# Feed-forward products of a two-layer transformer block by Strassen's scheme: seven block products for eight, all tokens in one pass over the weights

## The chip, the cores and the metric

The kernel runs on one core of a Trainium2 chip. The metric is device time in microseconds (us) for one execution; the median of three runs of the kernel before is 3087.64 us (3086.25 to 3088.11). Engines are named as in the profile: PE is TensorE (matmuls), PEld its weight loads, DVE is VectorE, ACT ScalarE, POOL GpSimd, SP SyncE (whose queue issues most transfers).

## What is computed

Two layers over 1024 latent tokens and 256 context tokens of width 1024, all in float32. Each layer has a conditioned norm, one input projection into three kinds of heads, an output projection, and then the part that is changed: a second norm and a gated feed-forward block of inner width 2816 (22 units of 128).

```python
def swiglu(h, w_in, w_out):
    g, u = jnp.split(h @ w_in, 2, axis=-1)
    return (jax.nn.silu(g) * u) @ w_out

# in each layer, after the heads:
x = x + g1[:, None] * y_l
x = x + g2[:, None] * swiglu(modulate(rms_norm(x, norm2[l]), sh2, sc2), w_ffn_in[l], w_ffn_out[l])
if not last:   # the context tokens go through the first layer's block only
    h_ctx = h_ctx + cg1[:, None] * y_c
    h_ctx = h_ctx + cg2[:, None] * swiglu(modulate(rms_norm(h_ctx, norm2[l]), csh2, csc2),
                                         w_ffn_in[l], w_ffn_out[l])
```

So the first layer's block has 1280 tokens, the second's 1024.

## The kernel before

Features lie on the 128 partitions, tokens along the free dimension. Every large product works on operands that are split into a rounded high part and a low part (`split`, L323: ScalarE casts the high part, VectorE subtracts for the low one), and takes three matmuls a k-tile (`part`, L473): high x high, high x low, low x high. A matmul's moving operand is a piece of tokens of one PSUM bank; `SUBS` (L201) gives the pieces: 320 + 320 in the first chunk of 640 tokens, 384 + 256 in the second. In the second layer the second chunk has only 384 latent tokens left, one piece.

The feed-forward block (`ffn`, L1772) goes through the chunks one after the other, first chunk 1, then chunk 0, and reads all of its weights for each. Per chunk it takes the 22 units in three groups (`FGROUPS`, L30). `ffn_group` (L1715) makes gate and up products of a unit, 8 k-tiles each, tanh on ScalarE, two multiplications on VectorE, and a split of the result, which stays in SBUF. `ffn_out` (L1740) then multiplies the 7 or 8 units of the group into each of the 8 output tiles, and VectorE adds each piece to x, which is in SBUF. Weight blocks come by `load_ahead` (L413, 3 raw buffers), are split by `split_ahead` (L431) one block ahead, and are taken by `take` (L460).

The order of every engine's instructions is the order in which the program issues them (`tc.manual_schedule()`). Side work (norms, the conditioning's vector products of this and the next layer) is kept in lanes; `pace` and `fill` (L285 to L301) put in a step of a lane wherever an estimate of each engine's clock says that VectorE and ScalarE are not ahead of TensorE by more than a slack. `finish` (L313) empties the lanes. The norm of chunk 0 for the block runs beside the last group of chunk 1, and in the first layer the next layer's first norm of chunk 1 runs beside the last group of chunk 0; the conditioning for the second layer (`conditioning_beside`, L570) is spread over both chunks of the first layer's block, with two sums on VectorE for each weight block. `running_rinv` (L634) sums the squares for a norm while x is written; `rms_rinv` (L484) makes the factor. `out_proj` (L1674) makes the output projection of one chunk. `final` (L1803) is the last norm.

Of the kernel before, what the change touches and what calls it, by code (L numbers as in the profile page):

```python
# [16 lines left out]
P = 128  # L17
D = 1024
# [11 lines left out]
FGROUPS = ((0, 8), (8, 15), (15, 22))  # L30

# Columns of the packed per-feature constants, per layer.
# [8 lines left out]
class _Line:  # L41
    """An estimate, kept while the kernel is traced, of when each engine is through with its work."""
# [26 lines left out]
    def note(self, engine, name, args, kw):  # L69
# [22 lines left out]
        if engine == "pe":  # L92
            # In columns: the engine has its full clock after a time in which it was busy enough.
# [10 lines left out]
class _Traced:  # L104
    """An engine of the core whose instructions are noted on the line."""
# [15 lines left out]
def hybrid_block_kernel(  # L121
# [28 lines left out]
    # Every engine runs its instructions in the order in which they are traced here.  # L150
# [3 lines left out]
    rp = ctx.enter_context(tc.tile_pool(name="raw", bufs=3))  # L154
    fp = ctx.enter_context(tc.tile_pool(name="full", bufs=27))
# [30 lines left out]
    def act(out, in_, func, **kw):  # L186
        """An activation; Ln and Exp keep to the one table set that has both where they meet."""
# [12 lines left out]
    # The columns (tokens) of each chunk in pieces of one PSUM bank; context: the last.  # L200
    SUBS = {0: ((0, 320), (320, 320)), 1: ((0, 384), (384, 256))}  # L201
# [23 lines left out]
    rope = cp.tile([P, SEQ], F32, name="rope")  # L225
# [14 lines left out]
    xs = dp.tile([2, 4, P, 2, CH], F32, name="xs")  # L240
# [44 lines left out]
    def fill(over=None):  # L285
        """Trace what steps of the lanes the engines have time for before the main stream's next one."""
# [29 lines left out]
    def alternate(main, side, every):  # L316
        """One step of side after every so many of main's."""
# [9 lines left out]
    # The weight blocks [P, k, m] in the order in which they are read: those that are split  # L327
    # (stationary operands of the large products) and the plain ones of the conditioning.
    plan = []

    # The input projection: its units, and the chunks that each pass over one takes.
    UNIT = dict(xr0=0, xr1=1, gg0=2, gg1=3, kv=4, qa0=5, qa1=6, su0=7, su1=8)
# [14 lines left out]
    # Of the conditioning's steps, those beside the first layer's projections, and those that come later.  # L347
    LATE = 8
    N_TICKS = 24 - LATE
    # What of the conditioning is computed beside the first layer's feed-forward: layer and block.  # L350
    BESIDE = [(0, 40), (0, 44)] + [(1, b) for b in range(0, 48, 4)]

    def pieces_of(l, c, name):
        """The pieces in which one unit of a chunk is computed."""
        return 2 if l < DEPTH - 1 or c == 0 or name in ("xr0", "xr1", "kv") else 1

    def plan_layer(l):
# [26 lines left out]
        for p in range(1, 4):  # L384
            # An even pair's values come with the next one's.
# [3 lines left out]
        ffn = []  # L389
        for c in (1, 0):  # L390
            for f0, f1 in FGROUPS:
                for f in range(f0, f1):
                    ffn += [(wfg_in[l, f], 8, P), (wfu_in[l, f], 8, P)]
                ffn += [(wfo_in[l, m, :, f0:f1, :], f1 - f0, P) for m in range(KT)]
        if l == DEPTH - 1:
            plan.extend(ffn)
        else:
            beside = [(wada_in[m, j], 2, 512) for m, b in BESIDE for j in range(b, b + 4)]
            u, n = FGROUPS[-1][0], FGROUPS[-1][1]
            pause = range(2 * u + 2 * KT, 2 * n + 3 * KT)  # L400
            plan.append(ffn[0])
            for i in range(len(ffn)):
                plan.extend(ffn[i + 1 : i + 2])
                if i not in pause:
                    plan.extend(beside[:1])
                    beside = beside[1:]
# [6 lines left out]
    def load_ahead():  # L413
        """Load the next block of the plan."""
        i = len(raws)
        if i < len(plan):
            src, k, m = plan[i]
            raw = rp.tile([P, k, m], F32, tag="wr", name=nm("wr"))
            sy.dma_start(raw, src)
# [11 lines left out]
    def split_ahead():  # L431
        """Split the next block, and load one more."""
# [9 lines left out]
    def split_first():  # L442
        """Split the first pair's weights, to a place of their own."""
# [1526 lines left out]
```

## Time and profile before

| | us |
|---|---|
| median of three runs | 3087.64 |
| profiled execution, first to last instruction | 3085.3 |
| first layer up to its output projection | 0 to 660 |
| first layer's output projection | 660 to 760 |
| first layer's feed-forward block | 760 to 1704 |
| second layer's heads | 1704 to 2240 |
| second layer's output projection | 2240 to 2326 |
| second layer's feed-forward block | 2326 to 3068 |
| last norm and stores | 3068 to 3085 |

Over the span TensorE is busy for 97%, VectorE for 60%, ScalarE for 47%, GpSimd for 13%; the mean granted clock is 0.984. The stages are read from the tables by stretch of time, the time of a single matmul from the chain of waits (a run of matmuls with its length and count, since the duration of one record includes a latency that overlaps the next one), and the time of an instruction of another engine from the groups by line and shape. Almost all rows name line 115, through which every instruction is issued; the tile names tell them apart: `ff` are the banks of gate and up products, `fo` those of output products, `wr`, `wh`, `wl` a weight block and its parts, `a` the gated products, `th` their making.

### The profile page before, as it was taken

The numbers are of one execution on the slowest core, as the hardware profiler recorded it, in microseconds if no ns is written. First come the engines' busy times: TensorE is split into PE (matmuls) and PEld (weight loads), VectorE is DVE, ScalarE is ACT, GpSimd is POOL, SyncE is SP. The second block draws the span as 40 slices with busy tenths as digits, with TensorE's granted clock in tenths as the row PEclk, the third lists the DMA queues.
The fourth block names the chain that finished last, engine by engine and source line by source line (L and its number), as shares of the span: only waits on it lengthen the run. The fifth ranks groups of instructions, "written<-read, shape, count | busy, mean of one in ns | idle before, by whom it ended". The sixth has DMA issues, their size and how long they took to land.

```text
span 3085.3 us, 44905 instructions
## 1 busy us (share of the span) xinstructions
PE 2997.7 (97%) x18205; PEld 2780.3 (90%) x18205; DVE 1842.0 (60%) x2992; ACT 1452.5 (47%) x2558; POOL 398.3 (13%) x342
## 2 busy tenths in 40 slices
PE   7999999999999999999999998999999999999997
PEld 4687687789999999999999887677799999999997
DVE  5785866666777764643355676766574457433334
ACT  5675788853322242222243676788743244312122
POOL 0001476600000000000000001467300000000000
PEclk8998999999999999999999998999999999999999
DMA  7312000032444433422223200000143443322222
GB/s 275 117 32 82 25 11 8 9 115 102 151 145 143 151 96 99 141 82 76 76 76 100 72 31 22 28 8 8 56 143 116 127 125 119 96 76 71 76 72 71
DMA packets 78672, 264.18 MB, mean 86 GB/s; under 512 B 8832, under 2 KB 16512, under 8 KB 78464
## 3 DMA queue, kind: packets, MB, share of 16 engines
q1 hardware_dynamic: 75840, 251.35, 25.5%
q0 software_dynamic: 2624, 9.96, 0.9%
q8 instruction: 142, 2.33, 0.3%
q14 instruction: 66, 0.54, 0.1%
HBM read 247.12 MB, written 14.16 MB: 85 GB/s over the span
## 4 chain that ended last, share of the span: by engine, by line
PE 78%; DVE 5%; ACT 3%; issue 1%; POOL 0%; DMA 0%; DVEq 0%; ACTq 0%; POOLq 0%
PE ff L115 36%; PE fo L115 18%; PE op L115 6%; PE pv L115 5%; PE s L115 5%; PE prj L115 3%; PE mx L115 1%; DVE mx L115 1%; PE sv L115 1%; PE q L115 1%; ACT pf L115 1%; PE ms L115 1%; DVE ql L115 0%; ACT ph L115 0%; PE adt L115 0%
## 5 line engine op out<-in xcount | busy, mean ns | idle before, releaser
L115 PE MATMUL ff<-h,wh 128*128 128x320 f32 (+2 forms) x4928 | 1106.3, 313 | 0.0
L115 PEld LDWEIGHTS ff<-h,wh 128*128 128x128 f32 x4928 | 834.7, 188 | 1.2
L115 PE MATMUL ff<-h,wl 128*128 128x320 f32 (+2 forms) x2464 | 769.8, 312 | 0.0
L115 PE MATMUL fo<-a,wh 128*128 128x320 f32 (+2 forms) x2464 | 552.4, 313 | 0.0
L115 ACT CAST wh<-wr 128x1024 fp32r<-128x1024 f32 (+1 forms) x338 | 344.4, 1019 | 409.6 <-PE fo L115 275.5
L115 DVE TENSOR_TENSOR wl<-wr,wh 128x1024 fp32r<-128x1024 f32 (+1 forms) x338 | 403.8, 1195 | 146.1 <-ACT wh L115 145.1
L115 PEld LDWEIGHTS ff<-h,wl 128*128 128x128 f32 x2464 | 463.6, 188 | 0.1
L115 PEld LDWEIGHTS fo<-a,wh 128*128 128x128 f32 x2464 | 417.2, 188 | 0.2
L115 PE MATMUL fo<-a,wl 128*128 128x320 f32 (+2 forms) x1232 | 384.9, 312 | 0.0
L115 POOL TENSOR_TENSOR pl<-pf,ph 128x512 fp32r<-128x512 f32 (+1 forms) x231 | 306.1, 1335 | 141.5 <-ACT ph L115 101.8
L115 PE MATMUL prj<-h,wh 128*128 128x320 f32 (+2 forms) x1056 | 252.5, 327 | 9.8 <-DVE h L115 3.8
L115 ACT CAST a<-th 128x320 fp32r<-128x320 f32 (+2 forms) x154 | 71.9, 467 | 392.6 <-DVE th L115 392.5
L115 ACT ACTIVATE pf<-s 128x512 f32<-128x512 f32 (+3 forms) x356 | 197.9, 564 | 110.9 <-PE s L115 106.2
L115 PEld LDWEIGHTS fo<-a,wl 128*128 128x128 f32 x1232 | 231.8, 188 | 0.0
L115 DVE SCALAR_TENSOR_TENSOR x<-fo,g2h,x 128x320 f32<-128x320 f32 (+2 forms) x168 | 94.1, 560 | 229.4 <-PE fo L115 228.2
L115 ACT ACTIVATE th<-ff 128x320 f32<-128x320 f32 (+2 forms) x154 | 68.5, 445 | 313.7 <-PE ff L115 313.5
L115 DVE SCALAR_TENSOR_TENSOR th<-th,ff 128x320 f32<-128x320 f32 (+2 forms) x154 | 76.3, 496 | 228.1 <-ACT th L115 227.5
L115 DVE TENSOR_REDUCE mx<-mx 128x1 f32<-128x512 f32 (+1 forms) x328 | 202.7, 679 | 16.3 <-PE mx L115 15.9
L115 PEld LDWEIGHTS prj<-h,wh 128*128 128x128 f32 x1056 | 183.8, 193 | 26.6 <-DVE h L115 7.8
L115 PE MATMUL op<-y,wh 128*128 128x320 f32 (+2 forms) x896 | 203.2, 315 | 0.8 <-ACT y L115 0.5
L115 PE MATMUL prj<-h,wl 128*128 128x320 f32 (+2 forms) x528 | 167.7, 318 | 2.0 <-DVE wl L115 2.0
L115 PE MATMUL s<-qh,kh 97*128 97x512 f32 (+5 forms) x356 | 158.9, 446 | 5.9 <-ACT qh L115 3.3
(239 smaller groups left out, 4497.8 us busy)
## 6 DMA issues: line engine op xcount, KB each, us to landing
wr<-in_wfg_dram SPq DMA_DIRECT2D x88, 512.0 KB, 3.7
wr<-in_wfu_dram SPq DMA_DIRECT2D x88, 512.0 KB, 3.7
wr<-in_wada_dram SPq DMA_DIRECT2D x80, 512.0 KB, 4.4
wr<-in_wfo_dram SPq DMA_DIRECT2D x64, 448.0 KB, 3.4
wr<-in_wout_dram SPq DMA_DIRECT2D x32, 512.0 KB, 3.7
wr<-in_wfo_dram SPq DMA_DIRECT2D x32, 512.0 KB, 3.6
wr<-in_win_dram SPq DMA_DIRECT2D x24, 512.0 KB, 3.6
x<-in_x_dram SPq DMA_DIRECT2D x16, 640.0 KB, 7.4
```

What stands on the lines that cost most here:

```text
L115: return f(*args, **kw)
```

## The change

The two chunks become two halves of equal size (640 and 640 tokens in the first layer, 512 and 512 in the second; pieces 384 + 256, or one piece of 512), and both go through the block in one pass over the weights.

`ffn_in`: for each unit the weights of gate and up, and for the tokens the two halves and the two halves of the features, are the blocks of a 2 x 2 by 2 x 2 block product. Winograd's form of Strassen's scheme takes seven products P1 to P7 of 4 k-tiles each instead of eight. The sums of weight blocks (S1 to S4) are made by GpSimd in the raw weights' place, four instructions of 512 elements, and each of the seven blocks is then split. The sums of token blocks (T1 to T4, with B11, B21, B22 the blocks themselves) are made once (`operands`) from the normed halves, and keep 28 large tiles. Three products share a bank (P1, P6 and P7, P4 add on one another), so a bank is copied or added to SBUF before the next product adds on it. The gated products go to a DRAM tensor `acts`; x after the output projection goes to a DRAM tensor `xm`, and comes back at the end of `ffn_in`.

`ffn_out`: the units are taken in fours (five groups of four; two units are left for plain products, `ffn_rest`). For each pair of output tiles seven products of 2 k-tiles; every bank is added to x after each product. `prepare` makes the weights' parts of a pair in two halves (a and b), `builder` the next group's operands out of `acts`. `either` chooses between GpSimd and VectorE by the estimated clocks.

The first layer's conditioning beside the block has three steps a unit, from the third unit on, and one sum instead of two where only the latents' values are used. The rotary table is loaded in each layer after the recurrences, the gates lie among the large tiles, which number 28 instead of 27, and raw weight buffers are 4 instead of 3. The last head's tokens are taken as 512 + 512 in the second layer. The core of the diff:

```diff
-FGROUPS = ((0, 8), (8, 15), (15, 22))
+QUAD = 4
+REST = NF // QUAD * QUAD
...
+        BLOCK = dict(P1="A11", P2="A12", P3="S4", P4="A22", P5="S1", P6="S2", P7="S3")
+        OPERAND = dict(P1="B11", P2="B21", P3="B22", P4="T4", P5="T1", P6="T2", P7="T3")
...
+        def either(out, a, b, op):
+            n = math.prod(out.shape[1:])
+            if line.clock["pool"] + n / 400 < line.clock["dve"] + n / 960 + 0.07:
+                gp.tensor_tensor(out, a, b, op=op)
+            else:
+                tt(out, a, b, op=op)
...
+        def ffn_in(ops, side):
+            early_order = ("P5", "P3", "P6", "P7", "P4")
+            order = ("P1", "P2", "P6", "P5", "P7", "P3", "P4")
+            seq = [(f, p) for f in range(EARLY) for p in order[:2]]
+            seq += [(f, p) for f in range(EARLY) for p in early_order]
+            seq += [(f, p) for f in range(EARLY, NF) for p in order]
...
+                split(hi, lo, src)
+                if p == "P2":
...
+                    gp.tensor_tensor(g1, g1, u1, op=OP.subtract)
+                    gp.tensor_tensor(u1, u1, u2, op=OP.add)
+                    gp.tensor_tensor(r["s2"], u2, g1, op=OP.subtract)
+                    gp.tensor_tensor(g2, g2, r["s2"], op=OP.subtract)
...
+            def product(f, p, wh, wl):
+                o = OPERAND[p]
+                ensure(lambda: o in ready)
+                key = dict(P1="A", P2="B", P5="C", P3="C").get(p, "A")
...
+        def tail(p):
+            if p == "P2":
+                load_acts((0, 2))
...
+            if p == "P5":
+                for kk in range(4):
+                    for c in (1, 0):
+                        sy.dma_start(xt[c][kk][:, :, :H], xm[kk, :, :, c * H : c * H + H])
...
+        def ffn_out():
+            load_acts((1, 3))
+            cur = {}
+            for _ in builder(0, cur):
+                pass
+            seq = [(gi, mp, part) for gi in range(len(groups)) for mp in range(4) for part in "ab"]
+            BLOCKS = dict(a=("P1", "P5", "P6", "P3"), b=("P7", "P2", "P4"))
...
+                if which == "a":
+                    r = wraw[gi, mp] = next_raw(False)
+                    a11, a12, a21, a22 = (r[:, 2 * q : 2 * q + 2, :] for q in range(4))
+                    split(hi[:, 0:2, :], lo[:, 0:2, :], a11)
+                    s = temp(512, name="s24").rearrange("p (k m) -> p k m", m=P)
+                    gp.tensor_tensor(a11, a11, a21, op=OP.subtract)
+                    gp.tensor_tensor(a21, a21, a22, op=OP.add)
+                    gp.tensor_tensor(s[:, 0:2, :], a22, a11, op=OP.subtract)
+                    gp.tensor_tensor(s[:, 2:4, :], a12, s[:, 0:2, :], op=OP.subtract)
+                    split(hi[:, 2:4, :], lo[:, 2:4, :], a21)
+                    split(hi[:, 4:8, :], lo[:, 4:8, :], s)
+                else:
+                    r = wraw.pop((gi, mp))
+                    split(hi[:, 0:4, :], lo[:, 0:4, :], r[:, 0:4, :])
+                    split(hi[:, 4:6, :], lo[:, 4:6, :], r[:, 6:8, :])
...
+                    for s0, n in HP:
...
+                        part(b, terms, first, True, not first)
                         fill(0.0)
+                        xp = x_part(c, m, s0, n)
+                        k = kind(c, s0)
+                        stt(xp, b, g2h[:, m, k : k + 1], xp, op0=OP.mult, op1=OP.add)
...
+                    if q == 0:
+                        prepare(i + 1)
+                    if mp == 3:
+                        cur.pop(o)
+                    if build is not None and (mp == 3 or (mp, p) in ((1, "P7"), (2, "P1"), (2, "P7"))):
+                        next(build, None)
```

At the layer's end `ffn_rest(1)` and `ffn_rest(0)` follow; in the first layer the next layer's norm of half 1 is issued beside `ffn_rest(0)`, and the next projection waits for it; in the second layer `final(1)` stands there, and `final(0)` at the end.

## Rows read from the trace of the kernel before

**Rows 1.** Tables by stretch: length, busy us (count) of each engine, clock, DMA, GB/s.

```profile
0.00:40.00 40.00, 20.63 (x102) 8.46 (x103) 19.14 (x51) 18.70 (x39) 0.70 (x7) 0.89 0.96 373
760.00:1704.00 944.00, 944.00 (x6461) 943.36 (x6460) 549.91 (x881) 281.84 (x441) 3.76 (x7) 1.00 0.35 111
1704.00:1740.00 36.00, 33.27 (x204) 30.00 (x203) 30.26 (x56) 19.03 (x36) 0.53 (x1) 1.00 0.22 69
2327.00:3068.00 741.00, 740.87 (x4756) 739.80 (x4755) 343.07 (x491) 229.75 (x342) 0.00 (x0) 1.00 0.31 94
```

**Rows 2.** Chain of waits, runs of matmuls: start us, us, what.

```profile
533.67 1.36 PE q L115 x6
760.54 42.22 PE ff L115 x288
1407.29 98.56 PE ff L115 x672
2326.27 66.59 PE ff L115 x384
```

**Rows 3.** Groups by line and shape, VectorE: busy us, mean ns | idle before.

```profile
L115 DVE TENSOR_TENSOR wl<-wr,wh 128x1024 fp32r<-128x1024 f32 x264 | 322.8, 1224 | 121.6 <-ACT wh L115 120.8 <-PE prj L115 0.9
L115 DVE SCALAR_TENSOR_TENSOR ada<-wr,cz,ada 128x512 f32<-128x512 f32 x196 | 134.5, 745 | 0.0
L115 DVE SCALAR_TENSOR_TENSOR x<-fo,g2h,x 128x384 f32<-128x384 f32 x48 | 29.6, 616 | 40.4 <-PE fo L115 40.2
L115 DVE TENSOR_TENSOR a<-th,a 128x384 fp32r<-128x384 f32 x44 | 24.6, 559 | 29.7 <-ACT a L115 29.7
L115 DVE SCALAR_TENSOR_TENSOR ht<-x,am,r 128x384 f32<-128x384 f32 x32 | 19.2, 612 | 0.1
L115 DVE SCALAR_TENSOR_TENSOR x<-fo,g2h,x 128x256 f32<-128x256 f32 x24 | 11.6, 484 | 36.0 <-PE fo L115 35.8
L115 DVE SCALAR_TENSOR_TENSOR ht<-x,am,r 128x256 f32<-128x256 f32 x24 | 11.3, 478 | 0.0
L115 DVE TENSOR_TENSOR a<-th,a 128x256 fp32r<-128x256 f32 x22 | 9.4, 426 | 10.4 <-ACT a L115 10.4
L115 DVE TENSOR_TENSOR rec<-rec,hr 128x512 f32<-128x512 f32 x8 | 5.5, 693 | 0.3
```

**Rows 4.** The same view, a cast of 512 elements on ScalarE.

```profile
L115 ACT CAST qh<-qf 128x512 fp32r<-128x512 f32 x16 | 10.0, 624 | 1.2 <-POOL qf L115 1.2
```

**Rows 5.** The same view, GpSimd.

```profile
L115 POOL TENSOR_TENSOR pl<-pf,ph 128x512 fp32r<-128x512 f32 x219 | 297.7, 1368 | 141.4 <-ACT ph L115 101.8 <-PE mx L115 22.4 <-PE s L115 3.7
L115 POOL TENSOR_TENSOR pl<-pf,ph 128x256 fp32r<-128x256 f32 x12 | 8.7, 744 | 0.1
```

**Rows 6.** Attention: two groups of VectorE, then the timeline (start us, us) of two engines.

```profile
L115 DVE TENSOR_TENSOR qf<-q,rope 32x512 f32<-32x512 f32 x32 | 21.9, 684 | 17.5 <-ACT qf L115 17.2
L115 DVE TENSOR_TENSOR att<-att,rd 128x512 f32<-128x512 f32 x12 | 20.4, 1702 | 0.0
...
579.76 2.78 DVE L115 TENSOR_TENSOR ql<-qf,qh 128x256 fp32r<-128x256 f32 x1
579.75 3.92 POOL L115 TENSOR_TENSOR pl<-pf,ph 128x512 fp32r<-128x512 f32 x3
```

**Rows 7.** Second layer's attention: stretches after a gap of TensorE, then its timeline.

```profile
1896.00:1900.00 4.00, 0.00 (x0) 0.00 (x0) 3.02 (x4) 3.97 (x5) 0.04 (x1) 0.80 0.00 0
1900.00:1912.00 12.00, 6.80 (x19) 5.54 (x20) 9.68 (x16) 1.66 (x4) 3.30 (x4) 0.50 0.00 0
1912.00:1916.00 4.00, 4.00 (x12) 3.09 (x12) 2.52 (x4) 3.26 (x5) 0.19 (x1) 0.57 0.00 0
...
1902.23 4.63 PE L115 MATMUL mx<-kh,qh 96*128 96x512 f32 x12 [7.52 <-ACT qh L115]
```

**Rows 8.** Chain of waits at the kernel's end, from the last square to the factor.

```profile
3072.16 0.41 DVE acc L115
...
3077.13 0.51 DVE r L115
```

More of the change, by code (lines that the diff above doesn't have):

```diff
@@ L585, in conditioning_beside @@
         for l, b in BESIDE:
-            accs = [temp(512, name="ada") for _ in (0, 1)]
+            both = l == 0 or b < 16
+            accs = [temp(512, name="ada") for _ in range(1 + both)]
             for j in range(4):
@@ L600, in conditioning_beside @@
                 yield
+            if not both:
+                rest.append((l, b, accs[0], ones[:, 0:2]))
+                continue
             acc, t = accs[0], temp(512, name="adh")
@@ L972, in recurrences @@
                     recurred.append(i)
+            gates.clear()
+            rope.append(full((P, SEQ), name="rope"))
+            sy.dma_start(rope[0], rope_in)
             Lane(recurrences_out(), 0)
@@ new lines, in two_deep, with build @@
+        def two_deep(seq, prepare):
+            units = [seq[i : i + 2] for i in range(0, len(seq), 2)]
+            built = {}
+            def build(u, i):
+                if u < len(units) and i < len(units[u]):
+                    if i == 0:
+                        built[u] = [wp.tile([P, 8, P], R32, tag=x, name=nm(x)) for x in ("wh", "wl")]
+                    hi, lo = (w[:, 4 * i : 4 * i + 4, :] for w in built[u])
+                    prepare(units[u][i], hi, lo)
+            for i in (0, 1):
+                build(0, i)
+            for u, unit in enumerate(units):
+                w = built.pop(u)
+                for i, item in enumerate(unit):
+                    build(u + 1, i)
+                    yield item, w[0][:, 4 * i : 4 * i + 4, :], w[1][:, 4 * i : 4 * i + 4, :]
+                if len(unit) == 1:
+                    build(u + 1, 1)
+                del w
@@ new lines, in builder, with rest_operands @@
+        def builder(f0, into):
+            sp_ = Split()
+            for p in ORDER2:
+                for i in range(QUAD // 2):
+                    quad_operands(f0, i, OPERAND[p], into, sp_)
+                sp_.flush()
+                yield
+        def rest_operands(into):
+            sp_ = Split()
+            for c in (1, 0):
+                for f in range(REST, NF):
+                    t = full((P, 2, CH), R32, "a")
+                    into[f, c] = t
+                    for s0, n in HP:
+                        sp_(*halves_of(t, s0, n), raw_a.pop((f, c, s0)))
+                sp_.flush()
+                yield
@@ new lines, in hybrid_block_kernel, with ffn_rest @@
+        rest = {}
+        def ffn_rest(c):
+            if c == 1:
+                for _ in (0, 1):
+                    raw = next_raw(False)
+                    hi, lo = (wp.tile([P, 8, P], R32, tag=x, name=nm(x)) for x in ("wh", "wl"))
+                    split(hi, lo, raw)
+                    del raw
+                    load_ahead()
+                    wrest.append((hi, lo))
+            for m in range(KT):
+                wh, wl = wrest[m // 4]
+                i = 2 * (m % 4)
+                for s0, n in HP:
+                    ps = psum("fr")
+                    prod(
+                        ps[:, :n],
+                        [
+                            (wh[:, i + j, :], wl[:, i + j, :], *halves_of(rest[REST + j, c], s0, n))
+                            for j in (0, 1)
+                        ],
+                    )
+                    fill(0.0)
+                    xp = x_part(c, m, s0, n)
+                    k = kind(c, s0)
+                    stt(xp, ps[:, :n], g2h[:, m, k : k + 1], xp, op0=OP.mult, op1=OP.add)
+                    written[c][s0] = m + 1
+                    if c == 0 and m == KT - 1:
+                        early[0] = 2.0
+                    yield
+                del wh, wl
+                if c == 0 and m % 4 == 3:
+                    wrest[m // 4] = None
+                    if m < KT - 1 or not last:
+                        ahead()
+            early[0] = 0.0
@@ L1833, in hybrid_block_kernel @@
+        Lane(first_operands(), 5)
+        pace(out_proj(0))
+        yts.clear()
+        if l == 0:
+            load_ahead()
+        assert used[0] == stops.pop(0)
+        stops.append(len(plan))
+        side = conditioning_beside() if l == 0 else None
+        pace(ffn_in(ops, side))
         finish()
         slack[0] = 0.0
+        if side is not None:
+            for _ in side:
+                pass
+        ts(g2h, mod[:, 40:48, :], 0.5, None, op0=OP.mult)
+        pace(ffn_out())
+        last_boxes = [None, None]
@@ L1839, in hybrid_block_kernel @@
+        last_boxes[0] = running(0, HP)
+        pace(ffn_rest(0))
+        rest.clear()
+        wrest.clear()
+        if last:
             Lane(final(0, last_boxes[0]), 0, True)
```

521 lines of the change are left out of this document (369 added, 152 removed).

## The prediction

> **What bounds the kernel now.** I read the stages first [rows 1]: in the first layer's feed-forward block TensorE is busy for all 944 us at the full clock (granted 1.00), in the second's for 740.9 of 741 us. VectorE is busy for 549.9 and 343.1 us of these stretches, GpSimd for 3.8 and 0. So only fewer or shorter matmuls can shorten them, and VectorE has some 390 us to spare in each layer. Then the chain of waits for the time that one matmul takes in a run of them [rows 2]: 42.22 us / 288 = 146.6 ns where pieces of 384 and 256 columns alternate, 98.56 / 672 = 146.7 ns with 320, 66.59 / 384 = 173.4 ns with 384, 1.36 / 6 = 226.7 ns with 512. That is 12.5 ns and 0.419 ns a column. Last I read what one instruction of VectorE, ScalarE and GpSimd takes at the widths of the change [rows 3 to 5].
>
> **TensorE's part.** A unit f has now 2 weight blocks x 8 k-tiles x 3 passes = 48 matmuls a piece of tokens, afterwards 7 products x 4 x 3 = 84 a piece of half the tokens. First layer, two pieces a half: 22 x 48 x 4 = 4224 become 22 x 84 x 2 = 3696; 528 x 0.1466 = 77.4 us less. Second layer: 1056 x 0.1734 + 2112 x 0.1467 = 492.9 us become 1848 x 0.2267 = 418.9, 74.0 less. The output products: 2112 become 5 x 4 x 7 x 12 + 192 = 1872 in the first layer, 35.2 us less; in the second 246.5 us become 936 x 0.2267 = 212.2, 34.3 less. The second layer's output projection (576 become 384 wider ones) gives 2.5. Sum: 223.4 us less. All of it lies on the path.
>
> **What stands in its place** is work for VectorE, ScalarE and GpSimd, and places where TensorE waits for it.
>
> **Output products, steady state.** A bank is added into x after each of the seven products: 7 x (0.616 + 0.484) = 7.7 us of VectorE for two output tiles in the first layer, 7 x 0.75 = 5.2 in the second (0.75 for 512 columns from the slope of the two) [rows 3]; before it was two additions a tile and piece, after 7 or 8 units each. TensorE has 84 x 0.1466 = 12.3 us and 42 x 0.2267 = 9.5 us for the same. Between these additions stands `prepare`, once for two tiles with a chain: low part of a11 on VectorE (0.43), four GpSimd subtractions or additions of 256 elements (4 x 0.744 = 3.0 [rows 5]) of which each needs the one before, ScalarE's cast of their result (0.62 [rows 4]), VectorE's low parts of it (0.69). The low part waits at the head of VectorE's queue, and behind it are queued the additions of P2, P4 and the next P1. In the second layer, from the end of P7's matmuls: 0.2 hop, 0.75 P7's addition, 0.43, 3.0, 0.62, 0.69 with hops 5.85, then 3 x 0.75 = 8.1 us. TensorE can meanwhile run P2, P4, P1 and P5 (4 x 1.36 = 5.44); P6 adds on the bank of P1, which must have been read: 2.65 us of waiting. P3 then waits 0.5 for P5's bank, behind two more low parts. 3.2 us x 20 = 63 us. In the first layer a product lasts 1.76 us: P6 is due at 4 x 1.76 = 7.04 and free at 5.6 + 2 x 1.10 + 0.62 = 8.4 (first piece), P3 is due at 10.2 and free at 10.6; 1.9 us x 20 = 38 us.
>
> Beside this the next group's operands are built: 28 low parts and 16 differences of 384 or 256 columns (44 x 0.49 = 21.6 us if VectorE has them all) in the first layer, 14 + 8 of 512 (15.2) in the second, or about twice that on GpSimd [rows 3, 5]. VectorE's own part of a group of four output pairs is already 30.8 + 11.1 + 13.6 of waiting = 55.5 of 57 us in the first layer, so what it gets lengthens the group. I take a third of it on VectorE, 6 us for each of the 4 groups of a layer that have a successor: 48. Together 149 us (38 + 63 + 48). Bounds: 27, if no chain waited and only the sum of the shared work counted (52.2 us for 49.2 and 41.8 for 38.1 in 8 groups), to 220, with 16 a group.
>
> **Start of each block.** Today the second half's norm lies beside the first half's last group. Now P1 and P2 of two units (4 x 3.52 = 14.1 us; 10.9 in the second layer) cover the other half's norm factor (5.5 us from the last square to the factor, as at the end of the kernel [rows 8]), then its operands: T1 needs per tile 1.09 + 2 x 0.99 + 0.99 = 4.05 us [rows 3], 16.2 for four; with 6 us of P2's evacuation and weight splits between it is ready at 28, TensorE wants it at 16: 12 us. B22 (15.5 with GpSimd's part), T2 (11.8), T3 (3.9) and T4 (11.8) each come against one product of 3.5 us, but overlap with one another on two engines; I take 18 more: 30 us, and 28 in the second layer, whose first two units also wait for a copy between two products on one bank. Bounds 12 and 44 each.
>
> **From the gated products to the output products.** The whole `builder` of the first group stands ahead of the first output weights in every queue, so TensorE waits for all of it. Transfers: 5.24 MB of x, three times 1.2 MB of activations and weights; at 373 GB/s [rows 1] 24 us, begun 17.6 us before the end; with landing 8 us after it. Then 21.6 us of differences and low parts and 2 us of weights: 32 us; second layer 8 + 15.2 + 1 = 24. Bounds 46 and 75 for both.
>
> **Gated products, steady state.** Per unit VectorE has seven low parts (7 x 0.69 = 4.8 us) and, in the first layer, seven instructions on the banks and their copies for each of two pieces (7 x 0.99 = 6.9): 11.7 us under TensorE's 84 x 2 x 0.1466 = 24.6, hidden. In the first layer the conditioning adds up to 3 x 4 x 0.745 = 8.9 us for 8 units, GpSimd's four sums of the weights 5.5: 26 of 24.6. I take 12 us in all (0 to 22). In the second layer nothing. Stores and loads of the products pass on SP's queue behind the weights; at 111 GB/s now [rows 1] there is room: nothing, cover the two blocks loaded ahead, up to 5 us without it.
>
> **Ends.** The last products of half 0 (14.1 us) now stand alone beside half 1's norm for the next layer: VectorE has 8 x (1.10 + 0.99) for additions and squares and 16 x 1.09 for the norm, 34 us; 20 us wait, two weight splits before the first product (1.22 each) and a later norm of half 0 add 4: 24 (12 to 32). Today's change of layer costs 36 - 33.3 = 2.7 us [rows 1]. The second layer's end: additions and squares 1.44 us a tile against 1.36 of TensorE, eight final scalings and one piece of 512 instead of 320: 8 (3 to 12). `rope`, loaded later, and GpSimd's stores of x are covered by the recurrences and the projection: nothing, 4 us a layer if they were not. **Clock.** After a gap of 7.52 us the granted clock was 0.50 (1.2 GHz) for 12 us and 0.57 for 4 [rows 7]; TensorE worked 6.80 + 4.00 us of these, so at most 5.4 us were lost. I take 4 us for each of the two long gaps ahead of the output products: 8 (0 to 25, if the starts and the shorter waits lower it too).
>
> Sum: -223.4 + 149 + 58 + 56 + 12 + 24 + 8 + 8 = +91.6. The profiled execution is 3085.3 us, the median of the runs 3087.6, 2.3 more: 3085.3 + 91.6 + 2.3 = 3179 us, 3.0% slower.
>
> **Where a rule bears on it.** In attention a low part of 128x256 on VectorE, 0.43 us elsewhere, took 2.78 us, begun 10 ns after three GpSimd instructions that lasted 3.92 [rows 6]; `att` x `rd` took 1.70 us on average where the same shape takes 0.69 [rows 3, 6]; products with one operand in PSUM held 0.684 [rows 6]. The Trainium skill (SBUF — State Buffer, Who interferes with whom) states that a VectorE instruction with two SBUF inputs and a GpSimd instruction that reads SBUF exclude each other for a whole instruction; the trace agrees. By that rule the operands that the change hands to GpSimd save no time.
>
> **Rivals.** (A) TensorE stays the bound in the output products: if `prepare`'s chain ended before P6 needs its bank (it decides at 5.44 us after P7 in the second layer and 7.04 in the first, against 8.1 and 8.4 worked out above), the stage costs 27 instead of 149: 3179 - 122 = 3057, faster. For it: VectorE's sum of work alone would fit, and an earlier start of GpSimd's four instructions would do it. Against: they write in place over what VectorE has just read, so can't start earlier. With the starts also at their lower bound 2980. Chance 0.25. (B) The blocking of rows 6 decides: differences and low parts on the two engines run one after the other, so a group costs 16 us instead of 6 (8 x 10 = 80) and a start 43 (26 more): 3285. For it: rows 6; against: GpSimd can work during the additions, which read PSUM. Chance 0.16. (C) The scheme doesn't save what it says because wider matmuls cost more a column: excluded by rows 2, no chance. Within 0.2% (about 6 us, what a measurement of this kernel can tell from no change): A and the forecast leave a gap there, 0.04. The forecast itself, 3100 to 3240, 0.55. So faster 0.25, same 0.04, slower 0.71; the range 3010 to 3300 leaves out A's lower part and B's upper, about 2 in 10.
>
> **What would show it.** Right: products of gate and up at 146.6 and 226.7 ns a matmul with hardly a gap; TensorE's busy share in the output products near 0.75 to 0.8, waits of `fo` matmuls for VectorE's `x`, VectorE waiting for ScalarE's `wh` behind GpSimd; two gaps of 20 us and more a layer, at the clock 0.5 after them. Wrong: output products near 246 us in the first layer, or operands ready before the two early units end. Most at risk is the order in which two engines share the operands.

## The result, and the profile after

The changed kernel takes 3354.4 us (median of 4 runs, 3353.4 to 3355.9), the kernel before 3087.5 in the same comparison: ratio 1.0865, 95% interval 1.0849 to 1.0880. The change loses 8.7%, where 3.0% was forecast. The profiled execution's span grew from 3085.3 to 3351.8 us, by 266.5.

The stages of the profile after, as in [rows 1] (length; busy us and count of TensorE, its weight loads, VectorE, ScalarE, GpSimd; clock; DMA; GB/s). First layer: output projection, start of the gate and up products to the end of the 14 early ones, their other 140, transition, output products. Second layer: start, the other products, transition, output products. In the second layer the start ends here, and in the runs below, with the 13th of the 14 early products, so 141 follow it. The projection's first matmul starts at 653.1 us, and at 642.9 before the change (not at 660, as the table ahead has it).

```profile
653.10:792.30 139.20, 125.30 (x781) 118.07 (x779) 88.57 (x169) 57.69 (x111) 0.00 (x0) 0.93 0.33 115
792.30:912.50 120.20, 74.91 (x339) 62.23 (x340) 77.76 (x121) 44.12 (x96) 53.38 (x51) 0.69 0.12 40
912.50:1417.10 504.60, 504.52 (x3474) 504.32 (x3472) 372.97 (x585) 170.12 (x352) 135.10 (x101) 1.00 0.41 139
1417.10:1443.80 26.70, 0.02 (x1) 0.02 (x1) 19.54 (x34) 10.54 (x27) 8.09 (x12) 0.58 0.48 150
1443.80:1788.70 344.90, 285.15 (x1681) 277.90 (x1682) 250.68 (x471) 94.61 (x220) 148.56 (x173) 0.88 0.19 60
2464.60:2551.30 86.70, 53.38 (x160) 33.05 (x159) 62.56 (x71) 34.38 (x57) 40.67 (x28) 0.72 0.10 37
2551.30:2961.20 409.90, 394.73 (x1692) 314.53 (x1692) 180.55 (x259) 133.21 (x239) 135.11 (x101) 1.00 0.26 90
2961.20:2981.90 20.70, 0.00 (x0) 0.00 (x0) 12.48 (x16) 7.83 (x14) 11.32 (x9) 0.57 0.54 181
2981.90:3299.70 317.80, 238.91 (x841) 178.65 (x842) 196.10 (x285) 79.36 (x161) 124.19 (x127) 0.85 0.16 53
```

Read each line against the time of its matmuls, at the durations that the chain of waits of the changed kernel shows for a product in one run (start us, us, what):

```profile
1002.26 3.51 PE ffA L117 x24
...
2950.29 2.72 PE ffC L117 x12
```

These are 146.3 and 226.7 ns a matmul, as in [rows 2]. The two starts need 14 x 3.515 = 49 and 13 x 2.72 = 35 us and take 120 and 87; the output products need 1680 x 0.1465 = 246 and 840 x 0.2267 = 190 and take 345 and 318. TensorE fills the first layer's long middle stage (504.5 of 504.6 us: 140 x 3.515 = 492 and 14 x 0.79 = 11 of conditioning, which lay in this block before too). In the second layer 141 x 2.72 = 384 us of products take 410.

The chain of waits in one pair of output tiles, first layer:

```profile
1455.40 0.48 DVE x L117
1455.88 0.34 DVE wl L117
...
1456.30 0.75 POOL wr L117
...
1457.11 0.73 POOL wr L117
1457.85 0.70 POOL s L117
...
1458.62 0.81 POOL s L117
...
1459.45 0.63 ACT wh L117
...
1460.10 0.69 DVE wl L117
1460.79 2.37 DVE x L117 x5
...
1463.30 2.02 PE foA L117 x12
```

This is the chain that the prediction worked out: an addition, a low part, four instructions of GpSimd, a cast, a low part, and only then the five additions queued behind it, for which TensorE waits. The page's row of these matmuls says how much:

```profile
L117 PE MATMUL foA<-T,wh 128*128 128x384 f32 (+2 forms) x720 | 212.8, 384 | 127.8 <-DVE x L117 127.8
```

### The profile page after: what moved, and what is told of

It reads as the page before. It is cut to its first block, busy times and chain, and to the rows that moved or that the text cites. A ratio compares the mean times of both kernels' runs of the same rounds, so it can differ in the third digit from the quotient of the medians.

```text
span 3351.8 us, 41619 instructions
## 1 busy us (share of the span) xinstructions
PE 2933.6 (88%) x15223; PEld 2495.7 (74%) x15223; DVE 2206.6 (66%) x3585; ACT 1561.4 (47%) x3013; POOL 1056.8 (32%) x938
## 4 chain that ended last, share of the span: by engine, by line
PE 44%; DVE 17%; issue 12%; POOL 8%; ACT 6%; DMA 1%; SPq 0%; POOLq 0%; DVEq 0%; ACTq 0%
PE ffA L117 9%; PE op L117 5%; PE pv L117 5%; PE ffC L117 5%; PE s L117 5%; DVE x L117 4%; POOL wr L117 4%; PE foA L117 3%; DVE wl L117 3%; POOL s L117 2%; PE prj L117 2%; PE foC L117 2%; PE ffB L117 2%; PE fr L117 1%; PE mx L117 1%
## 5 line engine op out<-in xcount | busy, mean ns | idle before, releaser
L117 DVE TENSOR_TENSOR wl<-wr,wh 128x512 fp32r<-128x512 f32 (+4 forms) x494 | 387.2, 792 | 247.8 <-ACT wh L117 245.2
L117 ACT CAST wh<-wr 128x512 fp32r<-128x512 f32 (+4 forms) x494 | 301.0, 621 | 422.7 <-PE foC L117 178.0
L117 PE MATMUL ffA<-T,wh 128*128 128x256 f32 (+2 forms) x1584 | 410.4, 344 | 44.4 <-ACT e L117 22.3
L117 PEld LDWEIGHTS ffA<-T,wh 128*128 128x128 f32 x1584 | 279.3, 192 | 83.0 <-ACT e L117 31.8
L117 PE MATMUL foA<-T,wh 128*128 128x384 f32 (+2 forms) x720 | 212.8, 384 | 127.8 <-DVE x L117 127.8
L117 PE MATMUL prj<-h,wh 128*128 128x384 f32 (+1 forms) x1056 | 261.0, 334 | 19.5 <-ACT h L117 8.5
L117 PE MATMUL ffA<-T,wl 128*128 128x384 f32 (+2 forms) x792 | 271.0, 342 | 0.5
L117 PE MATMUL op<-y,wh 128*128 128x384 f32 (+2 forms) x768 | 197.6, 344 | 2.5 <-ACT y L117 1.4
L117 PE MATMUL prj<-h,wl 128*128 128x384 f32 (+1 forms) x528 | 170.5, 323 | 7.7 <-DVE wl L117 7.7
L117 PEld LDWEIGHTS ffA<-T,wl 128*128 128x128 f32 x792 | 152.1, 192 | 18.5 <-DVE wl L117 8.8
```

The costliest lines, as they stand in the source:

```text
L117: return f(*args, **kw)
```

## The experiments

Their stage lengths are set against those above. Times of single runs, but for the last two; heads and attention, which none of them touches, scatter from 650 to 656 us in the first layer and 554 to 566 in the second, so stages are compared, not totals.

**Does the clock set the pace of the output products?** Twelve matmuls nobody reads, behind P5 of each pair:

```diff
+ for _ in range(12):
+     mm(fb[:, :fn], wh[:, 2 * q, :], fh, start=True, stop=True)
```

> The changed kernel with twelve extra matmuls (384 or 512 columns, into a bank that the next product overwrites) behind P5's product in each pair of output tiles, where TensorE then waits for VectorE's addition of P1. They do no useful work. Theory T: the waits of the output products lower TensorE's clock, and the low clock costs on top of them; of the 228 us that the two stages of output products take over their matmuls' time, 140 us are idle and 88 us matmuls at the low clock. With the extra matmuls the granted clock of the stages rises from 0.88 and 0.85 to 0.97 or more and the kernel gets 40 to 90 us faster (3265 to 3315). Rival R1: VectorE sets the pace, and matmuls at 1.2 GHz only fill time in which TensorE would wait anyway: clock up, time within 10 us of 3354.

3355.9 us. The two output stages:

```profile
1443.40:1792.90 349.50, 308.33 (x1921) 302.82 (x1922) 252.86 (x471) 94.70 (x220) 148.85 (x173) 0.95 0.19 59
2998.60:3302.30 303.70, 261.43 (x1081) 203.21 (x1082) 196.24 (x285) 79.52 (x161) 124.58 (x127) 0.98 0.17 56
```

The clock rose from 0.88 and 0.85 to 0.95 and 0.98, the stages changed by +4.6 and -14.1 us. In the second layer the clock is a small part of the surplus, 14 of 127 us; in the first it gives nothing back.

**What does the chain of sums cost?** GpSimd's four instructions of `prepare` left out.

```diff
- gp.tensor_tensor(a11, a11, a21, op=OP.subtract)
...
- split(hi[:, 4:8, :], lo[:, 4:8, :], s)
+ split(hi[:, 4:8, :], lo[:, 4:8, :], r[:, 4:8, :])
```

> The changed kernel without GpSimd's four sums of the output weights in prepare (the raw blocks are split instead, so the output products are of the wrong matrices); all matmuls, splits and additions stay. Theory T: the chain low part, four GpSimd sums, cast, low part at the head of VectorE's queue makes the waits (63 + 38 us of the 140 by the count of the prediction), and the clock follows: 110 to 190 us faster (3165 to 3245). Rival R2: what GpSimd and VectorE do to each other while they build the next group's operands sets the pace: 40 us or less faster (over 3310).

3217.4 us:

```profile
1444.90:1730.40 285.50, 256.95 (x1680) 252.73 (x1681) 247.53 (x467) 91.32 (x220) 92.99 (x97) 0.97 0.23 72
2925.70:3163.80 238.10, 207.45 (x841) 161.82 (x842) 196.07 (x281) 76.95 (x161) 69.81 (x51) 0.95 0.22 71
```

59.4 and 79.7 us less, with VectorE as busy as before (247.5 for 250.7, 196.1 both): what went is VectorE's waiting.

**Do the two engines block each other?** `either` always gives VectorE the work.

```diff
- if line.clock["pool"] + n / 400 < line.clock["dve"] + n / 960 + 0.07:
-     gp.tensor_tensor(out, a, b, op=op)
- else:
-     tt(out, a, b, op=op)
+ tt(out, a, b, op=op)
```

> The changed kernel with every operand's difference and low part on VectorE, none on GpSimd (the four weight sums stay on GpSimd). Rival R2 (the two engines block each other): 50 to 100 us faster. Theory T: the chain in prepare is as it was, VectorE has up to 12 us more in a group: same to 40 us slower (3350 to 3395) in the output products, with a few us back in the units of gate and up, where GpSimd's product no longer stands ahead of the weights' sums (28 us there in the second layer).

3337.8 us. The output products became 14.5 us longer in the first layer and 5.1 shorter in the second, the first start 5 us shorter, the second 1 us longer; so blocking does not decide in the output products, where 50 to 100 us less was expected of it. The second layer's gate and up stage fell from 496.6 to 471.6. Its reason stands in the timeline of a unit there after the change (start us, us, engine, instruction, [idle before]):

```profile
2654.48 1.68 POOL L117 TENSOR_TENSOR th<-th,e 128x512 f32<-128x512 f32 x1 [13.52 <-DVE th L117]
2656.12 1.29 POOL L117 TENSOR_TENSOR wr<-wr,wr 128x512 f32<-128x512 f32 x1
2660.06 0.62 ACT L117 CAST wh<-s 128x512 fp32r<-128x512 f32 x1 [5.87 <-POOL s L117]
2660.58 0.58 ACT L117 COPY e<-ffA 128x512 f32<-128x512 f32 x1
2661.21 0.74 PE L117 MATMUL ffA<-T,wh 128*128 128x512 f32 x2 [0.78 <-ACT e L117]
```

The product of the gated half waits on GpSimd for its factor, and the sums of the next unit's weights are queued behind it; ScalarE waits 5.87 us for their result, and behind that cast is queued the copy of P1's bank, on which P6 adds.

**Earlier sums.** Three sums out of place, half a pair earlier: 

```diff
+ s = wsum[gi, mp] = temp(512, name="s12").rearrange("p (k m) -> p k m", m=P)
+ gp.tensor_tensor(s[:, 0:2, :], a21, a22, op=OP.add)
...
```

> The changed kernel with three of the four weight sums out of place and issued half a pair earlier, so that they wait for no low part; the fourth (S4) stays behind the first split and is split last. The result is the same sum. Theory T: VectorE no longer waits 3.4 us in each of 40 pairs, TensorE's waits for the additions fall from 140 to 40 to 70 us and the clock of the stages rises: 100 to 180 us faster (3175 to 3255). Rival R2: 40 us or less faster.

3291.2 us: 324.9 (-20.0) and 268.6 (-49.2), about half of what leaving the sums out gave, and less than the 100 us or more that was expected: half a pair ahead, with the fourth sum left in its place, is not early enough.

**What is the rest?** The operands of the first group serve all five groups, and the others are neither loaded nor built:

```diff
- load_acts(range(groups[gi + 1], groups[gi + 1] + QUAD))
- build = builder(groups[gi + 1], following)
```

> Left out: in the output products of both layers the operands of groups 2 to 5 and their loads; all five groups use the first group's operands. The chain from GpSimd's sums over the cast and the split to the residual additions stays. The two output stages last 344.7 and 317.6 us after the change, of which the sums' chain was worth 59 and 80. Theory (the builder's work on VectorE and ScalarE is the second half of the surplus, on the path, and it adds to the chain): about 306 and 270, total about 3270. Rival (the chain alone sets the pace of a pair and the builder runs in the time that VectorE waits anyway): 340 and 313, total within 10 of 3354.

> Left out: the sums of weights and the operands of groups 2 to 5, both. Theory (these two are all of it): the stages come near the time of their matrix products, 250 and 195, total about 3130. Rival (a third cost, VectorE's splits of the weights and the residual additions, 28 of them in a group of four pairs, keep the stages above): 270 and 225 or more, total 3190 or more.

3245.2 and 3133.9 us. The output stages of the first run, then of the second:

```profile
1446.30:1722.00 275.70, 255.76 (x1681) 252.02 (x1682) 188.60 (x383) 48.78 (x108) 64.13 (x85) 0.98 0.14 44
2915.80:3191.10 275.30, 226.91 (x840) 177.53 (x841) 149.53 (x241) 47.96 (x105) 63.01 (x83) 0.87 0.12 39
```

```profile
1441.80:1690.10 248.30, 248.09 (x1681) 247.53 (x1682) 193.69 (x383) 46.60 (x108) 4.66 (x5) 0.99 0.16 49
2885.90:3080.40 194.50, 193.80 (x841) 157.70 (x842) 147.71 (x241) 46.00 (x105) 3.61 (x3) 0.99 0.17 55
```

Without both, TensorE is busy throughout: there is no third cost. Operands alone are worth 69.2 and 42.5, sums alone 59.4 and 79.7, both 96.6 and 123.3. In the second layer they add; in the first they overlap by 32 us, so the guess of 306 for the first run was too high there.

**Sums out of the way, two ways.** First the splits of the sums issued behind the next residual additions; with it, in the starts, each norm one piece ahead of its differences.

```diff
- split(hi[:, 4:8, :], lo[:, 4:8, :], s)
+ held.append((hi, lo, a21, s))
...
+ if q == 1:
+     release()
```

> Nothing is left out. Two edits in two stages. Output products: the casts and splits of the summed blocks are issued behind the residual additions of the next product but one, not ahead of them; GpSimd's sums stay where they are. Theory (VectorE's order makes the cost: residual additions, and with them the banks of PSUM, stand queued behind a split that waits for GpSimd): the two stages fall from 344.7 and 317.6 us to 290 to 310 and 255 to 275. Rival (the amount of work on VectorE and ScalarE, or the late operand itself, makes it): 335 or more and 305 or more. Start of the gate and up products: the norm of a piece is issued one piece ahead of its differences. If the serial pieces cost, the 14 early products end 8 to 14 us earlier in layer 0 (from 120.2) and 4 to 8 in layer 1 (from 86.7); if only the factor's arrival counts, nothing. Total 3230 to 3270.

Then all four sums out of place a whole pair ahead, and more lanes at once in the first layer's projection:

```diff
+ sums(i + 2)
- room[0] = 14
+ room[0] = 14 if last else 22
```

> Nothing is left out. Two edits in two stages. Output products: all four sums out of place and a whole pair ahead of their use. If lateness of the sums is the whole cost of the chain, the stages come to what they took without any sums, 285.5 and 238.1 (within 8); if GpSimd's work itself holds VectorE and ScalarE, they stay 15 or more above, near the 325 and 268.6 of three sums half a pair ahead. Layer 0's projection: lanes of weight 22 may run at once instead of 14, so that the running squares do not keep the heads' normalisation from beginning. If that was the cause of the waits of 2.5, 3.2 and 3.7 us, the stage falls from 139 to 122 to 128 with no new wait at its end; else 135 or more. Total 3220 to 3250.

The first took 3290.8 us with 310.2 and 289.2 in the output products: the order alone gives back 35 and 29, less than expected in the second layer. Its starts moved by -3.3 and +2.6 us, so that expectation fell. The second took 3233.0:

```profile
652.30:773.40 121.10, 116.80 (x781) 114.25 (x779) 88.35 (x169) 57.24 (x111) 0.00 (x0) 1.00 0.37 132
1430.80:1740.30 309.50, 265.71 (x1681) 259.43 (x1682) 250.81 (x437) 89.38 (x200) 166.49 (x187) 0.96 0.23 69
2940.20:3179.40 239.20, 209.39 (x841) 160.16 (x842) 201.56 (x256) 75.02 (x141) 149.79 (x136) 0.96 0.22 72
```

In the second layer it comes to what no sums at all gave (238.1): lateness was the chain's whole cost there. In the first it stays 24 us above (285.5) with VectorE busy for 81%; what makes these 24 is open. The projection fell from 139.2 to 121.1 us (before the change 117.5): 9.6 us of waits, and 8.5 us of the matmuls themselves, since the same 781 took 125.3 us at a granted clock of 0.93 and take 116.8 at 1.00. But the start behind it grew from 120.2 to 125.4, so 12.9 us remain; why it grew is open. After the change TensorE had these waits in its timeline in the projection, which are gone with the wider room: the lanes of `running` had kept the lanes that `finish_chunk` opens for its norm from beginning.

```profile
714.59 1.17 PE L117 MATMUL ms<-acc,ones 128*128 128x256 f32 x2 [2.54 <-DVE acc L117]
718.94 1.65 PE L117 MATMUL ms<-atsq,ones 128*128 128x384 f32 x2 [3.17 <-DVE atsq L117]
724.28 1.22 PE L117 MATMUL ms<-atsq,ones 128*128 128x256 f32 x2 [3.69 <-DVE atsq L117]
```

**The starts, and four moves.**

```diff
+ for name in ("B22", "T1", "T2", "T3", "T4"):
+     ops[name] = list(ops["B11"])
```

> Left out: the norm of the second half, the differences and sums of its operands and their splits; the five other operands are the first half's first block. The mean square of the second half is still taken. Theory (the operands' pieces, each one serial through VectorE, ScalarE and VectorE, make the long starts): the 14 early products end 55 to 62 us after the stage's start in layer 0 instead of 120, and about 40 in layer 1 instead of 87; total about 3245. Rival (the late block of weights and VectorE's order hold them): over 95 and over 70.

3255.1 us. The starts last 59.9 and 48.2 us: 60.3 of the first layer's 71 us of surplus and 38.5 of the second's 51 go with the operands (in the second about 40 us were expected to be left). Four moves, each read in its own stage; (i) begins the lanes of layer 0's first `running` behind `out_proj(1)`:

```diff
+ if l == 0 and c == 0 and m == KT - 1 and s0 == 0:
+     load_ahead()                 # (iv), ahead of the last store of x
+ prepare(0)                       # (ii), ahead of builder(0)
- either(a, a, u, OP.mult)
+ tt(a, a, u, op=OP.mult)          # (iii)
```

> Four moves in four stages, each read from its own stage. (i) Layer 0: the lanes that square x beside the first half of the output projection begin only behind it. If they held back the heads' normalisation, the projection's stage falls from 139 to about 118; if the stage is longer for the wider tiles, it stays. (ii) The first output weights are cast and split before the first operands: the two transitions of 27 and 21 us fall by 3 to 5 each if the weights stood behind the operands, else they stay. (iii) The product of the gated half goes to VectorE always: layer 1's stage of gate and up products falls from 496 by 20 to 25, layer 0's by 5 or less. (iv) Layer 0: the load of the next weight block is issued before the last store of the residual: the start of layer 0 (120 us to the end of its 14 early products) falls by 6 to 9 if the late block set it, by 0 if the operands' serial pieces do. Total 3300 to 3320.

3312.3 us, by stage. (i) 134.5 for 139.2 only; the waits in the middle are gone, but one stands at the end, where the norm is now late:

```profile
786.86 1.22 PE L117 MATMUL ms<-acc,ones 128*128 128x256 f32 x2 [15.09 <-DVE acc L117]
```

(ii) The transitions fell to 5.4 and 5.5, and the output products grew by 20.2 and 13.4: TensorE waits for the operands a little later instead. Net -1.1 and -1.8. (iii) 470.1 for 496.6, a little more than expected; the first layer's 140 products after the start kept their 504.6. (iv) The early products end 109.0 us after the stage's start, 11.2 earlier, but this run does not show what the move gives: by (i) the stage itself began later, 16.4 us after the projection's last matmul instead of 2.9. Counted from that matmul they end after 125.4 us, where it was 123.1. Projection and start together fell from 259.4 to 243.5. In the run of all moves below, which leaves (i) out, the matmuls of the norm's factor begin 5.8 us after the start instead of 9.9. Without the move the block's load stood behind the store of x on SP's queue, and ScalarE waited for it, VectorE for ScalarE, and the norm's factor behind both:

```profile
800.50 0.62 ACT L117 CAST wh<-wr 128x512 fp32r<-128x512 f32 x1 [7.77 <-DMA wr<-in_wfg_dram]
801.14 0.69 DVE L117 TENSOR_TENSOR wl<-wr,wh 128x512 fp32r<-128x512 f32 x1 [6.28 <-ACT wh L117]
```

**What of the operands sets the start?** Matmuls that nobody reads, ahead of the terms that wait (120 a layer, as the counts below show; the expectation says 110):

```diff
+ for _ in range(FILL[p][j]):
+     mm(fb[:, :256], x[:, 0, 0:P], x[:, 0, 0:256], start=True, stop=True)
```

> Nothing is left out; added are 110 matrix products a layer whose result nobody uses, ahead of the terms of the early products that wait for operands. In layer 0's start the 14 products keep TensorE busy for 75 us instead of 49, at granted clocks of 0.57 to 0.72 in its first 100 us. If the clock is on the path there, it rises and the 14 end 10 to 20 us earlier in layer 0 and 5 to 12 in layer 1. If the operands' arrival is, they end within 4 us of 120.2 and 86.7, and the total stays within 6 of 3354.

3356.2 us, and the two starts:

```profile
789.30:909.50 120.20, 90.53 (x459) 81.26 (x460) 77.84 (x122) 44.31 (x99) 53.45 (x51) 0.76 0.12 40
2461.30:2550.70 89.40, 65.04 (x280) 48.28 (x279) 61.96 (x71) 34.74 (x60) 40.45 (x28) 0.89 0.10 36
```

The clock rose from 0.69 and 0.72 to 0.76 and 0.89; the starts stayed at 120.2 and went from 86.7 to 89.4. While TensorE waits for operands its low clock is not on the path, though it makes 49 us of products into 75. Behind the last wait it can be, by little: the 15 matmuls there take 4.24 us in both runs, where 146 ns each make 2.2. Then the opposite test:

```diff
- tt(t, t, lo, op=OP.subtract)
...
- either(x22, x22, lo, OP.add)
...
- either(t, t, lo, OP.add)
```

> Left out, in the starts alone: the subtraction or addition of the low half in the operands T1, T2 and T4 (24 instructions in layer 0, 12 in layer 1; in layer 0's start these lines hold VectorE for about 11 us and GpSimd for 6). Theory (the amount of work that VectorE and GpSimd do in line for the operands sets the start, neither the clock nor the order of the products): the 14 early products end 9 to 16 us earlier in layer 0 (120.2) and 5 to 10 in layer 1 (86.7), about what is left out. Rival (the arrival of the norm's factor and of the weights sets it): within 3 in both.

3336.1 us; the starts end 10.3 and 6.7 us earlier, about the time of the instructions left out. It is the work in line on VectorE and GpSimd.

**All moves together.** Sums a pair ahead, lanes of 22, (iii), (iv), early products of both units in turn, half of the first group's operands built inside the last unit.

```diff
- seq += [(f, p) for f in range(EARLY) for p in early_order]
+ seq += [(0, "P5"), (1, "P5"), (0, "P3"), (1, "P3"), ...]
...
+ quad_operands(0, 0, OPERAND[p], cur, sp_)
```

> Nothing is left out. The sums a pair ahead, lanes of weight 22 in layer 0's projection, the gated product on VectorE and the early load, as in the runs before, and two new edits. Start: the early products of the two units alternate (P5, P5, P3, P3, ...) instead of unit by unit. If the waits for operands (42 us in layer 0) can be filled with the second unit's products (5 of 3.5 us), the 14 end 92 to 100 us after the stage's start in layer 0 (120.2 before the edit, some 109 by the early load alone) and 72 to 80 in layer 1 (86.7); if VectorE's work on the operands sets the end, 105 or more and 83 or more. Transitions: half of the first group's operands is built inside the last unit of gate and up products. If that work was exposed, 26.7 and 20.7 us fall to 8 to 12 without the output stages becoming longer than 309 and 239 by over 5; if it comes back there, as it did in the run of four moves, the sum of both stays. Total 3130 to 3175 by the theory, 3185 to 3200 if neither edit gives anything.

> As e12_all_moves, with the low halves of the first group's operands taken before their tile is overwritten (in that run, in layer 1, they were taken after). The same instructions in a slightly other order on VectorE and GpSimd: total 3173, within 6.

3173.3 and 3176.0 us, the second 1.0291 of before (1.0261 to 1.0321). The starts last 108.4 and 83.1 us in the first of the two. In the first layer the run of four moves is no measure for the alternation, since its stage began late; the run with the sums a pair ahead is, with the same projection and a start of 125.4. The last part of T4, first there, then here (the stages begin at 773.4 and 773.1):

```profile
876.68 1.02 DVE L117 TENSOR_TENSOR T<-t,T 128x256 fp32r<-128x256 f32 x1 [0.61 <-ACT T L117]
874.65 0.80 POOL L117 TENSOR_TENSOR T<-t,T 128x256 fp32r<-128x256 f32 x1 [1.40 <-ACT T L117]
```

The last operand is ready 104.3 and 102.4 us after the stage's start, and from then to the end of the 14 products 21.1 us pass without the alternation and 6.0 with it. So filling TensorE's waits gave some 15 us; the end then lies where the operands end, and these came hardly earlier, which is why 92 to 100 was not reached. In the second layer the start became 3.6 us shorter. The transitions fell to 5.3 and 4.1 in the second run, and its output products rose from the 309.5 and 239.2 of the sums a pair ahead to 325.7 and 251.3, most of it back. So about two thirds of the loss is to be had back; no version here beats the kernel before.

## Why the prediction was right or wrong

The direction, and the chain that makes it, were right; the size was about a third (91.6 of 266.5 us). Two steps failed: the waits in the starts, and the price of the operands built beside the output products. By its terms, forecast against measured:

| term | forecast us | measured us |
|---|---|---|
| TensorE | -223.4 | as forecast: 146.3 and 226.7 ns a matmul |
| output products, waits | 149 | 98.7 + 127.4 = 226 |
| starts | 30 + 28 | 71 + 51.3 = 122 |
| transitions | 32 + 24 | 26.7 + 20.7 = 47 |
| gated products, steady | 12 + 0 | 1 + 26 |
| ends (second layer's heads 528.7 to 554.0; after the last product 17.4 to 27.5) | 24 + 8 | 25 + 10 |
| projection, first layer (117.5 to 139.2) | 0 | 22 |
| heads, first layer (642.9 to 653.1) | 0 | 10 |

Measured: -223 + 226 + 122 + 47 + 27 + 35 + 22 + 10 = 266, the span's 266.5. The term for the clock, 8, has no line of its own: what the clock cost lies inside the others. Fillers that raised it changed stages by 0, +2.7, +4.6 and -14.1 us; where TensorE waited for little, in the first layer's projection, the low clock cost 8.5.

*Output products.* The chain was found and placed rightly, its price was too low: 101 forecast (38 + 63), 139 measured by leaving the sums out (59 + 80). The second layer's is the larger, as worked out. The operands' share was the worse guess: "a third of it on VectorE, 6 us" a group, 48 in all, where leaving them out gave 69 + 43. The stated reason for more, a group already full on VectorE (55.5 of 57 us), was in the text; the bound of 16 a group fits it better than 6 (69 + 43 in 8 groups are 14). With their overlap of 32 us the two make 220, the very end of the bounds (27 to 220). That bound was added up too low: 16 a group make 38 + 63 + 128 = 229.

*Starts.* This step left its bounds (44 each at most). T1 was to be ready after 28 us, and the four operands behind it were given 18 us of waiting because they "overlap with one another on two engines". The last parts of T1 and of T4 in the first layer, whose stage begins at 792.3:

```profile
839.91 0.42 DVE L117 TENSOR_TENSOR T<-t,T 128x256 fp32r<-128x256 f32 x1 [0.47 <-ACT T L117]
890.75 0.73 POOL L117 TENSOR_TENSOR T<-t,T 128x256 fp32r<-128x256 f32 x1 [0.52 <-ACT T L117]
```

T1 was ready after 48.0 us: its first difference began 21.5 us after the stage, and a tile took 5.6 us instead of 4.05, where VectorE's waits for ScalarE (0.59 + 0.47 + 0.68 us a tile in its timeline) had no price. The other four then took 51.2 us, more than the 43.0 that the prediction's own prices (15.5 + 11.8 + 3.9 + 11.8) make one after the other. So nothing was gained by two engines. VectorE and GpSimd at 868 us:

```profile
868.27 5.63 DVE L117 TENSOR_TENSOR T<-x,T 128x256 fp32r<-128x256 f32 x5 [0.55 <-ACT T L117]
868.01 5.61 POOL L117 TENSOR_TENSOR T<-x,T 128x384 fp32r<-128x384 f32 x5 [1.04 <-ACT T L117]
```

Five instructions each in the same 5.6 us: the VectorE ones last 1.13 us where this shape took 0.426 [rows 3]. This is rival B's blocking, and the Trainium skill's rule (SBUF — State Buffer, Who interferes with whom) shows in these rows. With all of this work on VectorE the first start was 5 us shorter and the second 1 us longer. B's cause was wrong in the output products, though: in the first layer GpSimd's share saves 14.5 us, since without it the stage grew by that.

*Second layer's units.* "In the second layer nothing" failed: the sum of VectorE's work was right and leaves room, but nobody asked what stands ahead of GpSimd's sums in its queue. One product of 1.68 us that waits there cost all of the 26 us: with it on VectorE the gate and up products took 470.1 instead of 496.6.

*Projection.* The prediction has no term for the first layer's. Its matmuls are as many as before, but the change adds two lanes of weight 4 to a room of 14, and the prediction did not follow which lanes may begin in it.

*Right, or nearly:* transitions (operands stand ahead of everything, and so (ii) gained nothing), both ends, TensorE's saving. Rival A named earlier sums as what would turn the sign. With them the second layer lost its chain, but its stage kept 49 us above its matmuls and the first 63, where A had 27 for both, and the total stayed 144 us above before: the operands were the part that A left out. A's lowest time was also added up wrongly: with both starts at 12 us it is 3057 - 34 = 3023, not 2980. The 10 us in the first layer's heads were not explained: every run of the changed kernel has 650 to 656 us there, the one trace of before 642.9.

## What to carry to other kernels

Where TensorE is busy for all of a stage, a scheme that cuts its work is priced by what the other engines must do in order: count the sums and splits per engine, and for each that waits name what is queued behind it, on GpSimd too. Price the ramp (first operands of a stage) instruction by instruction on one engine, without credit for a second one that shares its operands' path. And move work with the wait in view: four moves here gave at least part of a gap back one stage later.

## What the runs showed of the hardware

A low granted clock cost nothing in the first start, where TensorE waited for others: at 0.69 its 14 products took 75 us instead of 49, and at 0.76, with 120 matmuls more, the stage still ended after 120.2. Where it waited for little the clock did cost: the 781 matmuls of the first layer's projection took 125.3 us at 0.93 and 116.8 at 1.00. Two engines that subtract side by side ran at the rate of one: 1.13 us for VectorE's 128x256, for as long as GpSimd's five instructions lasted.
